# Two-layer hybrid encoder on one core: the transfers that sum the down weights, issued from GpSimd behind marks

## The chip, the cores and the metric

The kernel runs on one core of a Trainium2 chip. The core has five engines that run side by side, each with its own in-order queue: TensorE (PE, with its weight loads shown apart as PEld), VectorE (DVE), ScalarE (ACT), GpSimd (POOL) and SyncE (SP), which only issues transfers. Transfers run on 16 DMA engines, whoever issues them. The metric is the time of one execution on the device in microseconds (us).

## The reference

Two layers of a bidirectional encoder over 512 tokens of width 1024, all in float32. Each layer is a half-step feed-forward block (SwiGLU, inner width 2816), a mixer with three kinds of attention, and a second half-step feed-forward block, each between two RMS norms:

```python
for l in range(DEPTH):                       # 2
    y = swiglu(rmsnorm(h, ffn1_pre_g[l]), ffn1_w_gu[l], ffn1_w_down[l])
    h = h + 0.5 * rmsnorm(y, ffn1_post_g[l])
    u = rmsnorm(h, mix_pre_g[l])
    proj = u @ w_in[l]                       # q, k, v of A, B, C and the gates
    ...                                      # oa, ob, oc: three attentions
    yb = jnp.einsum('bsnc,ncd->bsnd', branches, w_branch[l])
    merged = jnp.sum(gates * yb, axis=2)
    h = h + rmsnorm(merged @ w_out[l], mix_post_g[l])
    y = swiglu(rmsnorm(h, ffn2_pre_g[l]), ffn2_w_gu[l], ffn2_w_down[l])
    h = h + 0.5 * rmsnorm(y, ffn2_post_g[l])

def swiglu(x, w_gu, w_down):
    gate, up = jnp.split(x @ w_gu, 2, axis=-1)
    return (jax.nn.silu(gate) * up) @ w_down
```

## The kernel before, in words

A product in float32 is made as three matmuls of a high and a low part (`mm3`, lines 291 to 293, and `unit`, line 1002): every weight tile is fetched (`wr`, three buffers, 512 KB each), copied to a high part by ACT (line 199) and to a low part by DVE (line 200), both in one buffer of tag `wp`, of which there are four.

The kernel is four feed-forward blocks and two mixers, in the order ffn(0,1), mixer 0, ffn(0,2), ffn(1,1), mixer 1, ffn(1,2). A feed-forward block computes its first `plain` of 22 rows of the inner layer straight (6 in the first block, 4 in the others), and the rest in `count` groups. Each group makes a gate and an up row by seven products of half size, a Strassen-like scheme (`product`, line 783, 84 matmuls of 256 columns in a group). Its weights are two `wr` tiles fetched by SP (`fetches`, line 186), summed and split on DVE and ACT (`sum13` line 637, `low1` line 645, `low24` line 674 and their like). `gated` (line 851) writes a row of activations at the end of a group. In the first block alone `keep` (lines 720 to 723) also turns the input by 32 transposes and stores it to memory (`kept<-h`, SP).

The down projection uses the same scheme, and there sums of weight quarters are wanted: `s3`, `s2`, `s1` and `s4`. They are not made on an engine but in memory. `sum_up(l, which)` returns 32 steps for a block: four sums, each of four copies (`begin_sum`, line 252, from the weights or from an earlier sum into a tile `sum`) and then four additions (`add_to`, line 256, a transfer from GpSimd's queue that adds into that tile), 512 KB each. All tiles `sum` have memory of their own. Later the sums are read like other weights (line 869).

Who calls the steps: `begin` of the first block fills `stream["beside"]` with the 32 steps of ffn(0,1), and the group loop takes three of them at a time (line 981). The mixer of layer l makes a list `todo` of the steps for ffn(l,2) and, in layer 0, for ffn(1,1) too, 64 and 32 steps, and spreads them over its own 77 steps (`ORDER`, line 1460). The place in the program is only where a step is traced: a scheduler writes each engine's order, outside of the regions under `ordered()`, by when it expects an instruction to be ready, and a copy of weights from memory is ready at once.

In a mixer GpSimd also multiplies for the rotary embedding: `rope` (lines 1247 to 1256) copies a projection on ACT, shifts it through four small SP transfers (`sh<-raw`), multiplies by a table on GpSimd (line 1255) and adds on DVE (line 1256). `combine` adds branches on GpSimd (line 1408).

Of the kernel before, what the change touches and what calls it, by code (L numbers as in the profile page):

```python
# [34 lines left out]
KP = KF - 2 * KS  # L35
# [74 lines left out]
def encoder_kernel(ctx: ExitStack, tc: tile.TileContext, order, xT, wts, cols, rows, rpb, consts, tables, out):  # L110
    nc = tc.nc
# [19 lines left out]
    def nm(s):  # L131
        serial[0] += 1
        return f"{s}{serial[0]}"

    def big(tag, dt=F32, shape=(P, T), name="v"):
        if tag in BUFS:
            return sb.tile(list(shape), dt, tag=tag, name=nm(name), bufs=BUFS[tag])
        kind, pool = phase[0]
        return pool.tile(list(shape), dt, tag=tag, name=nm(name), bufs=ABUFS[kind][tag])

    def small(tag, w=4, bufs=4):
        return sb.tile([P, w], F32, tag=tag, name=nm(tag), bufs=bufs)
# [4 lines left out]
    V, A, G, PE = nc.vector, nc.scalar, nc.gpsimd, nc.tensor  # L147

    def f(t):
        return t.bitcast(F32)  # L150
# [21 lines left out]
    stream = {"raw": [], "ready": [], "made": 0, "held": {}, "limit": 0, "stop": NTILES * 2, "later": [], "pace": 1, "eng": nc.scalar, "beside": []}  # L172
# [57 lines left out]
    extra, down, sums = [], {}, {}  # L230
# [5 lines left out]
    for l in range(L):  # L236
        for which in (1, 2):
# [3 lines left out]
            for key, (r, c) in places.items():  # L241
                src = wts[(NSTREAM + len(extra)) // WB].rearrange("p (a b) -> p a b", a=2)
# [3 lines left out]
    def sum_up(l, which):  # L246

        steps = []

        def begin_sum(key, old, u):  # L250
            t = dr.tile([P, 2, T], F32, tag="sum", name=nm("sum"), bufs=L * 2 * 4 * (KS // 2))
            nc.sync.dma_start(t, down[l, which, (old, u)] if old in ("21",) else sums[l, which, (old, u)])
            sums[l, which, (key, u)] = t

        def add_to(key, more, u):
            G.dma_start(sums[l, which, (key, u)], down[l, which, (more, u)], accum_op=ALU.add, max_dma_last_dim=4096)

        for key, old, more in (("s3", "21", "11"), ("s2", "s3", "22"), ("s1", "21", "22"), ("s4", "s2", "12")):
            steps.extend((lambda key=key, old=old, u=u: begin_sum(key, old, u)) for u in range(KS // 2))
            steps.extend((lambda key=key, more=more, u=u: add_to(key, more, u)) for u in range(KS // 2))  # L260
        return steps

    G.memset(ones, 1.0)
    G.memset(epst, EPS)
# [30 lines left out]
    def dense(blocks, X, tags=("mm",), i=None, accs=None, ws=None, midway=None, hooks={}):  # L295
        accs = accs or [bank(tags[n % len(tags)]) for n in range(len(blocks))]
        kept = []
        for k in range(len(X)):
            if midway and k == len(X) // 2:
                midway()  # L300
            x = X[k] if i is None else (X[k][0][:, i, :], X[k][1][:, i, :])
            for n, (acc, (name, l, r0, c)) in enumerate(zip(accs, blocks)):
                w = ws[k * len(blocks) + n] if ws else wblk(name, l, r0 + k, c)
                kept.append(w)
                mm3(acc if i is None else acc[:, HALVES[i]], w, x, k == 0, k == len(X) - 1)
            if k in hooks:
                hooks[k]()
        return (accs, kept) if i == 0 else accs

    def dense1(name, l, c, X, r0=0, tag="mm", midway=None):  # L310
        return dense([(name, l, r0, c)], X, (tag,), midway=midway)[0]
# [196 lines left out]
    def ffn(l, which, X, accs):  # L508
# [4 lines left out]
        plain = 6 if first else 4  # L513
# [39 lines left out]
        acts, low2, few = {}, [None, None], []  # L553
        PH, PL = [], []

        def place(m):
# [13 lines left out]
                acts[m] = low2[1][k // HK][:, :, k % HK, :]  # L570
            return acts[m]

        def settle(u):

            for parts in (PH, PL):
                if u < 2:
                    t = sb.tile([P, 2, T], F32R, tag="wp", name=nm("part"), bufs=BUFS["wp"])
                    parts.append([t[:, 0, :], t[:, 1, :]])
                else:
                    parts.append([big("t", F32R, name="part") for _ in range(2)])  # L580
            for k in range(2):
                p, q, a = PH[u][k], PL[u][k], few[0][:, 2 * u + k, :]
                A.activation(p, a, AF.Copy)
                V.tensor_tensor(out=q, in0=a, in1=f(p), op=ALU.subtract)
# [3 lines left out]
        def finish(m, pg, pu):  # L588
            t = big("t", name="t")
            if first:  # L590
                v = big("t", name="v")
                V.tensor_tensor(out=t, in0=pg, in1=rB, op=ALU.mult)
                A.activation(t, t, AF.Silu)
                V.scalar_tensor_tensor(out=v, in0=pu, scalar=-1.0, in1=rB, op0=ALU.mult, op1=ALU.mult)
                V.tensor_tensor(out=place(m), in0=t, in1=v, op=ALU.mult)
            else:
                A.activation(t, pg, AF.Silu)
                V.scalar_tensor_tensor(out=place(m), in0=pu, scalar=-1.0, in1=t, op0=ALU.mult, op1=ALU.mult)
# [154 lines left out]
        finish(1, g1, u1)  # L753
        for m in range(2, plain):
            finish(m, dense1(gu, l, m, X.blocks), dense1(gu, l, KF + m, X.blocks, tag="at"))
        while later:
            later.pop(0)()
        if first:
# [169 lines left out]
        for g in range(count):  # L928
            more, last = g + 1 < count, g + 1 == count
            p1(g)  # L930
            if g:
                add22(g - 1)
            low24(g)
            if more:
                high1(g + 1)
            seed(g)
            if more:
                sum13(g + 1)
            p7(g)
            if more:  # L940
                high13(g + 1)
                low1(g + 1)
            copy7(g)
            if g:
                p3(g - 1)
            if more:
                sum2(g + 1)
            else:
                preps(1)
            if g:  # L950
                silu1(g - 1)
            if more:
                high12(g + 1)
            if g:
                gated(g - 1)
            p6(g)
            if more:
                low13(g + 1)
            else:
                preps(2)  # L960
            copy2(g)
            p4(g)
            add21(g)
            if last:
                p5(g)
                add22(g)
                t3(0)
            p2(g)
            silu0(g)
            if more:  # L970
                low12(g + 1)
                sum4(g + 1)
                fetches(g + 2)
                p5(g)
                high24(g + 1)
            if g == count - 3:
                cut("1", "11", 0)
            if g == count - 2:
                cut("1", "11", 1)
                loads(3)  # L980
            for _ in range(3):
                if stream["beside"]:
                    stream["beside"].pop(0)()
        assert not stream["beside"]
        region = ordered()
        region.__enter__()
# [114 lines left out]
        for s, (kind, u) in enumerate(seq):  # L1101
# [28 lines left out]
            elif kind == "3" and u == 0:  # L1130
# [7 lines left out]
                for tb in range(2):  # L1138
# [4 lines left out]
                    t = kept_v["v12"][:, tb, :]  # L1143
# [115 lines left out]
    def mixer(l, op, first):  # L1259
        w, X = "w_in", op.blocks  # L1260
        todo = sum_up(l, 2) + (sum_up(l + 1, 1) if l + 1 < L else [])
# [7 lines left out]
        for c0, n in ((0, 512), (512, 384)):  # L1269
            m = big("g", name="mask")  # L1270
# [158 lines left out]
        def do(u):  # L1429
            kind, i = u[:2], int(u[2:] or 0)  # L1430
            if kind == "qa":
                if i == 0:
                    held[u] = qkv_a(*first)
                else:
                    early = second if i == 1 else []
                    late = [dense1(w, l, c + i, X) for c in (QA, KA, VA)[len(early) :]]
                    held[u] = qkv_a(*early, *late)
            elif kind == "kb":
                held["kb"] = qkv_b(KB), turn(plain(dense1(w, l, VB, X), False), 2)
            elif kind == "qb":  # L1440
                held[u] = qkv_b(QB + i)
            elif kind == "qc":
                held[u] = qkv_c(i)
            elif kind == "aa":
                attn_a(i, *held.pop(f"qa{i}"))
            elif kind == "ab":
                attn_b(i, held.pop(f"qb{i}"), *held["kb"])
            elif kind == "ac":
                attn_c(*held.pop(f"qc{i}"))
            elif kind == "fc":  # L1450
                finish_c(i)
            elif kind[0] == "g":
                gates("abc".index(kind[1]), i)
            elif kind[0] == "y":
                combine("abc".index(kind[1]), kind[1], i)

        steps = ORDER.split()
        for n, u in enumerate(steps):
            do(u)
            while todo and len(todo) * (len(steps) - 10) > (len(steps) - 10 - n) * todo_n:  # L1460
                todo.pop(0)()
        assert not todo
        M = [split(merged[m], "st", 0.5) for m in range(KD)]

# [113 lines left out]
```

## Time and profile before

| What | Value |
|---|---|
| median of 3 runs | 2659.02 us (2656.55 to 2659.67) |
| the profiled execution | 2658.71 us, span 2656.9 us |
| PE, PEld busy | 2466.7 us (93%), 2165.6 us (82%) |
| DVE, ACT, POOL busy | 1766.8 us (66%), 1349.2 us (51%), 139.6 us (5%) |
| mean granted PE clock | 0.965 |
| moved by transfers | 390.93 MB, mean 147 GB/s |

The profile is of one execution. The page gives, for each of 40 equal slices of the span (66.4 us), one digit, the busy share in tenths. Other views group the instructions by line or by the tile that they write, list who waited for whom, follow the chain of work that ended last back from the end, and give the queues of the DMA engines, where q0 holds GpSimd's transfers, q1 SP's and q10 ACT's. A busy PE is not PE at its peak, since matmuls overlap: how long a run of them takes is read from the chain.

### The profile page before, as it was taken

To read this page: it belongs to the slowest core of one execution; us is meant where nothing else is said; L and a number is where in the kernel's file an instruction comes from. 1 tells how busy PE (TensorE), PEld (TensorE's weight loads), DVE (VectorE), ACT (ScalarE), POOL (GpSimd) and SP (SyncE) were. 2 spreads that over 40 slices of the span, in tenths; PEclk is the share of its full clock that TensorE was granted. 3 is DMA by queue.
4 is the path that set the end of the run, shared out by engine and by line. 5 is a ranking of instruction groups with operands and counts; after the bars stand their busy time and mean duration, and the time that the engine had idled before them with its cause. 6 is when DMAs were issued, how large, how long until landed. Compare 5 with 4: busy or idle time off the path is not lost.

```text
span 2656.9 us, 37791 instructions
## 1 busy us (share of the span) xinstructions
PE 2466.7 (93%) x14298; PEld 2165.6 (82%) x14298; DVE 1766.8 (66%) x2903; ACT 1349.2 (51%) x2471; POOL 139.6 (5%) x128
## 2 busy tenths in 40 slices
PE   7367799899999999999999999989999999999997
PEld 6257798788887787999878999877888778799986
DVE  6144577667676655788766787657577574678784
ACT  4122355455555545555555556446555454555553
POOL 1111100000001110000000000000001111000000
PEclk9678899999999999999999999999999999999999
DMA  9999946364453333333542335636344433333452
GB/s 283 270 292 287 245 130 228 110 179 108 118 154 106 110 102 113 98 103 110 198 159 96 104 104 170 202 121 168 108 120 130 120 111 102 98 111 104 135 185 93
DMA packets 129430, 390.93 MB, mean 147 GB/s; under 512 B 17504, under 2 KB 24288, under 8 KB 128224
## 3 DMA queue, kind: packets, MB, share of 16 engines
q1 hardware_dynamic: 98000, 275.18, 32.3%
q10 hardware_dynamic: 22032, 79.78, 9.9%
q0 software_dynamic: 9216, 33.56, 6.6%
q8 instruction: 112, 1.84, 0.3%
q14 instruction: 70, 0.57, 0.1%
HBM read 335.50 MB, written 81.79 MB: 157 GB/s over the span
## 4 chain that ended last, share of the span: by engine, by line
PE 69%; DMA 13%; DVE 9%; ACT 4%; issue 2%; SPq 1%; POOL 1%; DVEq 0%; ACTq 0%; POOLq 0%
PE mm L783 20%; PE mm L1002 7%; PE mm L293 7%; PE mm L292 7%; PE mm L291 7%; DMA sum<-in_wts_dram 6%; PE at L1002 4%; PE at L783 3%; DMA wr<-in_wts_dram 3%; PE at L293 2%; PE at L292 2%; PE at L291 2%; PE o L1002 2%; DMA sh<-raw 1%; DMA braw<-in_rpb_dram 1%
## 5 line engine op out<-in xcount | busy, mean ns | idle before, releaser
L291 PE MATMUL mm<-X,w 128*128 128x512 f32 (+1 forms) x998 | 386.1, 387 | 2.4 <-ACT w L199 1.2
L292 PE MATMUL mm<-X,w 128*128 128x512 f32 (+1 forms) x998 | 386.0, 387 | 0.0
L293 PE MATMUL mm<-X,w 128*128 128x512 f32 (+1 forms) x998 | 384.6, 386 | 0.0
L200 DVE TENSOR_TENSOR w<-wr,w 128x512 fp32r<-128x512 f32 x366 | 258.9, 714 | 186.5 <-ACT w L199 183.1
L199 ACT ACTIVATE w<-wr 128x512 fp32r<-128x512 f32 x366 | 226.5, 627 | 239.9 <-PE mm L293 176.7
L783 PE MATMUL mm<-ht,h 128*128 128x256 f32 x1120 | 323.4, 289 | 16.1 <-ACT at L822 13.5
L783 PE MATMUL mm<-lt,h 128*128 128x256 f32 x1120 | 322.2, 288 | 0.0
L783 PE MATMUL mm<-ht,l 128*128 128x256 f32 x1120 | 322.1, 288 | 0.0
L783 PE MATMUL mm<-X,h 128*128 128x256 f32 x1120 | 213.3, 288 | 44.5 <-DVE v L837 44.5
L783 PEld LDWEIGHTS mm<-ht,h 128*128 128x128 f32 x1120 | 220.9, 197 | 17.1 <-ACT at L822 14.1
L783 PEld LDWEIGHTS mm<-lt,h 128*128 128x128 f32 x1120 | 221.0, 197 | 0.0
L783 PEld LDWEIGHTS mm<-ht,l 128*128 128x128 f32 x1120 | 220.5, 197 | 0.0
L291 PEld LDWEIGHTS mm<-X,w 128*128 128x128 f32 x998 | 190.9, 191 | 33.9 <-ACT w L199 1.4
L783 PEld LDWEIGHTS mm<-X,h 128*128 128x128 f32 x1120 | 179.0, 196 | 46.0 <-DVE v L837 45.7
L293 PEld LDWEIGHTS mm<-X,w 128*128 128x128 f32 x998 | 190.6, 191 | 31.6
L292 PEld LDWEIGHTS mm<-X,w 128*128 128x128 f32 x998 | 191.0, 191 | 31.0
L1002 PE MATMUL mm<-wh,f 128*128 128x512 f32 x640 | 199.7, 390 | 0.0
L783 PE MATMUL mm<-X,l 128*128 128x256 f32 x560 | 161.0, 287 | 0.0
L637 DVE TENSOR_TENSOR r<-wr,wr 128x1024 f32<-128x1024 f32 x70 | 85.5, 1221 | 87.5 <-DMA wr<-in_wts_dram 83.6
L1002 PEld LDWEIGHTS mm<-wh,f 128*128 128x128 f32 x640 | 120.2, 188 | 25.0
L645 DVE TENSOR_TENSOR l<-wr,h 128x1024 fp32r<-128x1024 f32 x70 | 85.7, 1225 | 80.9 <-PE mm L783 80.9
L1002 PE MATMUL mm<-wl,f 128*128 128x512 f32 x320 | 125.0, 391 | 3.6 <-DVE wl L880 3.6
(348 smaller groups left out, 5463.4 us busy)
## 6 DMA issues: line engine op xcount, KB each, us to landing
wr<-in_wts_dram SPq DMA_DIRECT2D x187, 512.0 KB, 3.6
wr<-in_wts_dram ACTq DMA_DIRECT2D x152, 512.0 KB, 3.7
sum<-in_wts_dram POOLq DMA_DIRECT2D x64, 512.0 KB, 18.2
sum<-in_wts_dram SPq DMA_DIRECT2D x32, 512.0 KB, 10.4
sum<-sum SPq DMA_DIRECT2D x32, 512.0 KB, 7.6
ht<-sum SPq DMA_DIRECT2D x32, 512.0 KB, 4.3
lt<-sum SPq DMA_DIRECT2D x32, 512.0 KB, 4.4
ht<-in_wts_dram SPq DMA_DIRECT2D x28, 512.0 KB, 4.5
```

The source lines that it names most:

```text
L199: A.activation(hi, raw, AF.Copy)
L200: V.tensor_tensor(out=lo, in0=raw, in1=f(hi), op=ALU.subtract)
L291: PE.matmul(acc, w[0], x[0], start=start, stop=False)
L292: PE.matmul(acc, w[0], x[1], start=False, stop=False)
L293: PE.matmul(acc, w[1], x[0], start=False, stop=stop)
L637: V.tensor_tensor(out=W[g]["r13"], in0=base, in1=raws[g][0], op=ALU.add)
L645: V.tensor_tensor(out=W[g]["l1"], in0=raws[g][0], in1=f(W[g]["h1"]), op=ALU.subtract)
L783: PE.matmul(acc, ws[i], xs[j], start=start and k == n == 0, stop=stop and k == HK - 1 and n == 2, skip_group_check=True,)
L1002: PE.matmul(acc, x[i], w[j], start=start and n == 0, stop=stop and n == 2, skip_group_check=True)
```

## The change

The copies that begin a sum are issued by GpSimd, on the queue of the additions, in place of SP. A new function `paced` makes a mark on GpSimd, a copy of one column (128 x 1) of data that the running step has just made, and puts the transfers that it is given behind that mark in GpSimd's order (`issue_after` orders the issue on that engine and adds no other wait). In the first block two steps go behind a row of activations after each of the four plain rows from m = 2, and two after each group from g = 1, so that the 32 steps end with the 16th pair. In the mixers the steps that fall due after a step of `ORDER`, mostly one in mixer 0 and one in every second step in mixer 1, go behind a mark read from the low part of the weight tile that was used last.

```diff
         def begin_sum(key, old, u):
             t = dr.tile([P, 2, T], F32, tag="sum", name=nm("sum"), bufs=L * 2 * 4 * (KS // 2))
-            nc.sync.dma_start(t, down[l, which, (old, u)] if old in ("21",) else sums[l, which, (old, u)])
+            G.dma_start(t, down[l, which, (old, u)] if old == "21" else sums[l, which, (old, u)])
             sums[l, which, (key, u)] = t
...
+    def paced(calls, src):
+
+        mark = G.tensor_copy(small("mark", 1, 2), src)
+        with tc.issue_after(mark.ins):
+            for call in calls:
+                call()
...
+        def beside(src):
+            if stream["beside"]:
+                paced(stream["beside"][:2], src)
+                del stream["beside"][:2]
...
         for m in range(2, plain):
             finish(m, dense1(gu, l, m, X.blocks), dense1(gu, l, KF + m, X.blocks, tag="at"))
+            beside(acts[m][:, 0:1])
...
-            for _ in range(3):
-                if stream["beside"]:
-                    stream["beside"].pop(0)()
+            if g:
+                beside(acts[plain + g - 1][:, 0, 0:1] if plain + g > KP else acts[plain + g - 1][:, 0:1])
...
         for n, u in enumerate(steps):
             do(u)
+            ready = []
             while todo and len(todo) * (len(steps) - 10) > (len(steps) - 10 - n) * todo_n:
-                todo.pop(0)()
+                ready.append(todo.pop(0))
+            if ready:
+                paced(ready, f(stream["tile"][1])[:, 0, 0:1])
```

## The prediction

> **What bounds the kernel now.** I read the page first: busy shares by slice, and the transfers' share under them.
>
> ```profile
> span 2656.9 us, 37791 instructions
> ...
> PE   7367799899999999999999999989999999999997
> ...
> DMA  9999946364453333333542335636344433333452
> ```
>
> TensorE's digit is 8 or 9 everywhere but in the first five slices of 66 us and at the very end, and in those five the 16 DMA engines are full. So I asked for busy time in stretches: the first feed-forward block up to its last product (15 to 390), then the two mixers, with a later feed-forward block between them.
>
> ```profile
> 15.00:390.00 375.00, 258.13 (x1703) 242.50 (x1702) 184.86 (x259) 125.71 (x212) 52.28 (x64) 0.82 0.92 256
> ...
> 530.00:1045.00 515.00, 505.88 (x2464) 414.65 (x2462) 335.83 (x753) 278.08 (x604) 43.44 (x29) 1.00 0.44 125
> 1045.00:1260.00 215.00, 212.32 (x1627) 206.42 (x1628) 167.29 (x214) 119.27 (x194) 0.00 (x0) 0.98 0.34 102
> ...
> 1760.00:2255.00 495.00, 484.63 (x2379) 397.68 (x2380) 322.56 (x724) 264.59 (x570) 43.49 (x29) 0.99 0.44 125
> ```
>
> The columns are length, busy time of PE, PEld, DVE, ACT and POOL, granted clock, DMA share, GB/s. In the first block PE is idle for 117 us of 375 and its clock is 0.82. In the other three stretches PE is busy 98% of the time with DMA at 0.34 to 0.44. What fills the DMA engines is told by the tile `sum`:
>
> ```profile
> L256 POOL DMA_DIRECT2D sum<-in_wts_dram x64: 805/814/976, 24.2 to 302.1; - x64
> L252 SPq DMA_DIRECT2D sum<-in_wts_dram x32: 488/581/1156, 15.3 to 268.9; - x32
> L252 SPq DMA_DIRECT2D sum<-sum x32: 467/474/607, 31.9 to 290.3; - x32
> ```
>
> All 128 transfers of all four feed-forward blocks, 64 additions and 64 copies, start between 15 and 302 us, though three of the blocks need theirs only much later. The waits of that stretch say whom this hurts:
>
> ```profile
> DVE r L637 <- DMA wr<-in_wts_dram: 78.0, 11, 18.4
> ...
> PE o L720 <- ACT h L722: 50.9, 3, 30.5
> DVE t L592 <- DMA kept<-h: 45.3, 2, 38.3
> PE mm L783 <- DVE v L837: 44.5, 6, 15.0
> ...
> SPq L252 <- DMA sum<-in_wts_dram: 146.8, 23, 30.9
> ```
>
> The last row is SP's queue: for 146.8 us it stood at a copy that waited for an addition to land, and the stores `kept<-h` and the loads `wr` stood behind it. PE's two waits, 50.9 and 44.5 us, are the ends of those two chains.
>
> **What stage one would take without it.** PE's work that is left at 60 us comes from a row of busy time for line 293 alone, the transposes' row, and three links of the chain that ended last:
>
> ```profile
> 60.00:150.00 90.00, 16.58 (x38) 8.13 (x38) 0.70 1.02 274
> ```
>
> ```profile
> L720 PE MATMUL o<-cons,a x32: 270/296/475, 55.5 to 126.4; 128*128 128x128 f32 x32
> ```
>
> ```profile
> 377.16 10.08 PE mm L783 x84
> 387.24 1.45 PE at L783 x12
> ...
> 428.03 23.12 PE mm L1002 x102
> ```
>
> Of line 293's matmuls 38 come after 60 us, and as many of 291 and 292: 114 of 512 columns. In an unbroken run 102 of that width take 23.12 us, 0.227 each: 25.8 us. A product matmul takes 10.08/84 = 0.12 us; the 32 transposes at the same price make 3.8. A group is 84 products, 10.08 us, and there are 16 groups (22 rows less 6 plain ones): 161.3. So 60 + 25.8 + 3.8 + 161.3 = 251 us, against 388.7 (387.24 + 1.45) now. At most **137.7 us** can be had.
>
> **What the DMA engines would have to carry.** Two answers on the queues and issues, the first of a quiet stretch (1100 to 1250), the rest of a full one (160 to 300):
>
> ```profile
> q1 hardware_dynamic: 4359, 15.89, 34.6%
> ...
> wr<-in_wts_dram SPq DMA_DIRECT2D x30, 512.0 KB, 3.6
> ```
>
> ```profile
> q0 software_dynamic: 4332, 15.77, 59.0%
> q1 hardware_dynamic: 3144, 24.50, 45.1%
> ...
> sum<-in_wts_dram POOLq DMA_DIRECT2D x32, 512.0 KB, 18.2
> wr<-in_wts_dram SPq DMA_DIRECT2D x16, 512.0 KB, 11.8
> sum<-sum SPq DMA_DIRECT2D x16, 512.0 KB, 9.7
> sum<-in_wts_dram SPq DMA_DIRECT2D x14, 512.0 KB, 13.2
> ```
>
> A weight load costs all 16 engines 0.346 x 150/30 = 1.73 us. An addition: 0.59 x 140 us over 15.77/0.524 = 30 of them, 2.74 us. The copies share q1 with 16 loads: 0.451 x 140 - 16 x 1.73 = 35.4 us over 30, 1.2 us each. Three blocks' 48 additions and 48 copies leave stage one: 131.5 + 57.6 = 189 us of engine time, of 0.92 x 375 = 345. What stays, 156 us, fits into 251 at a share of 0.62, so PE becomes the bound. The stores and loads lose the queue in front of them; next late is a load that meets a pair of sums.
>
> **The pairs that stay (16 of them).** Four run beside the plain products, twelve beside groups. The groups have little room, as the chain and VectorE's order show:
>
> ```profile
> 277.46 12.13 DMA wr<-in_wts_dram
> ...
> 294.05 11.37 DMA wr<-in_wts_dram
> ...
> 311.12 7.91 DMA wr<-in_wts_dram
> ```
>
> ```profile
> 1152.05 1.23 DVE L645 TENSOR_TENSOR l<-wr,h 128x1024 fp32r<-128x1024 f32 x1 [1.56 <-PE mm L783]
> 1153.19 0.69 DVE L851 TENSOR_TENSOR a<-t,v 128x512 f32<-128x512 f32 x1
> ```
>
> From load to load it is 16.59 and 17.06 us, of which the load 12.13 and 11.37; the rest (sum, splits, release of the buffer) is 4.5 to 5.7, say 5.1. A group of 10.08 us is kept if a load lands within 5.0 us; quietly it takes 3.6. The release is L645's end, and L851, whose output the mark reads, comes right behind it: the pair of sums and the load always meet. If they don't slow each other: 0. If the load waits for the whole pair: 3.6 + 2 x 2.74 + 5.1 = 14.2 for an addition pair (+4.1), 3.6 + 2.4 + 5.1 = 11.1 for a copy pair (+1.0), six of each: 31 us. The load starts ahead and both interleave, so I take half: **15 us**. The four plain pairs stand beside loads issued two tiles ahead: 3 us, ends 0 and 10. Stage one ends at 251 + 18 = 269: **-119.7 us**.
>
> **The parts with one answer.** SP loses 64 issues of some 0.5 us; POOL gains them at an addition's 0.81, 64 x 0.81 = 52 us over stretches where it is busy 43 of 515 or, with the additions gone elsewhere, not at all: nothing on PE's path. The 112 marks (16 + 64 + 32) read one column each; the nearest POOL rows are an issue, 0.81, and the 1.3 of a whole tile below, and I take 0.2; POOL's idle time hides them. In the first block only sums stand behind a mark. An addition waits for a copy issued two pairs (some 20 us) earlier in the groups, four steps in a mixer, and copies land in 9.7 even when all is full: no wait.
>
> **The mixers.** The first gets 64 transfers: 32 x 3.94 = 126 us of engine time, share 0.44 to 0.68; the second 32: 0.44 to 0.57. PE has 2% to spare. Behind POOL's new work stands the rotary step. First who waits for it (line 1256 on VectorE: us, times), then one such link of the chain, then two of POOL's multiplies in order of time:
>
> ```profile
>   POOL sh L1255: 24.2, 14
> ```
>
> ```profile
> 833.83 3.57 DMA sh<-raw
> 837.55 1.30 POOL sh L1255
> ```
>
> ```profile
> 697.67 1.29 POOL L1255 TENSOR_TENSOR sh<-sh,sinR 128x512 f32<-128x512 f32 x1 [36.01 <-DMA sh<-raw]
> ...
> 762.15 1.28 POOL L1255 TENSOR_TENSOR sh<-sh,sinR 128x512 f32<-128x512 f32 x1 [13.62 <-DMA sh<-raw]
> ```
>
> 14 of the 26 rotary steps are waited for. At worst each meets an issue in front of it (0.81) and an addition beside its `sh` transfer (2.74): 14 x 3.55 = 50 us. At best none does: 0. A transfer is in flight a quarter of the time in the first mixer (126/515) and POOL is issuing a tenth: 14 x (0.25 x 2.74 + 0.1 x 0.81) = **11 us**. Each mark also holds a weight buffer (`wp`, four of them) until POOL has read it; a buffer lasts PE 12 matmuls, 2.7 us, so four hold 10.9, and the low part that the mark reads is written before PE uses it. I take nothing; if that cover goes, see the last rival.
>
> **Sum.** The profiled execution took 2658.7 us (span 2656.9), 0.3 under the median of 2659.0. 2658.7 - 119.7 + 11 = **2550 us**.
>
> The Trainium skill's page "DMA: Bandwidth & Descriptors", section "Issuing engines are not separate DMA queues", says that issuing from several engines "will only save the time on the sequencer it takes to initiate the DMA". By it the move to POOL alone is worth SP's 64 issues, about 32 us off the path, and all gain has to come from the delay; SP's 146.8 us row speaks for more, since a wait on the queue moves along with the issue. The same page ("SWDGE vs HWDGE vs iDMA") calls SP's path the faster to set up, and says that GpSimd writes its descriptors where VectorE can lock it out. That speaks against the change; the issues' 805 to 976 ns beside a VectorE busy half the time show little of it, and by its figures to the first byte, about 1 us against 0.6, 64 copies would be 26 us later in all, beside other work.
>
> **Rivals.** (a) The stage stays bound by transfers: its own sums cost the full 31 + 10 us, and some stores stay late; PE's wait goes to `wr` again. The overlap of L645 and L851 speaks for it, a share of 0.62 against. 2658.7 - 137.7 + 41 + 11 = 2573, to 2590 if a third of the 50.9 us wait stays. (b) The mixers pay in full: 50 us instead of 11, 2589. For it speaks their 2% of slack, against it that transfers are in flight only a quarter of the time. (c) Slower: marks keep weight buffers. POOL works in order; a mark queued behind a rotary multiply that waits for its transfer (36.0 and 13.6 us above) is read late, the split of a later tile can't start, PE stops. With 13.6 us of wait and 8 of cover (three buffers), each of 26 steps costs 5.6: 146 us, more than the 119.7 won, 2685. It decides from 4.6 us a step. Against it: those waits are mostly idle time, in which a mark may go first. (d) The marks don't hold the transfers back, as their data come early: 2658. Against it: in the mixers the data are that step's weights, which can't be there in stage one.
>
> **How the numbers follow.** Main case 0.63 (2521, the full 137.7 with free mixers, to 2572), (a) 0.17, (b) 0.12, (c) 0.06, (d) 0.02. Range: 2520 to 2605, which takes in (a), (b) and a mix of their bounds; main case's own 2521 to 2572. Faster by over 0.2% 0.92, within 0.2% (about what a measurement of this kernel can tell from no change) 0.02, slower 0.06.
>
> **What would show it.** Right: about 30 `sum` issues before 280 us, the rest inside the mixers; the DMA digit falls to 6 or 7 in the first four slices and rises in the first mixer; last L783 at 260 to 285; `DVE t <- kept` gone; `wr` landing in 4 to 7 us beside pairs. The forecast is wrong if `wr` waits stay above 40 us in stage one, if PE's idle time in the mixers grows past 60 us, or if ACT's split (L199) waits for POOL.

## The result and the profile after

The changed kernel takes 2569.86 us (median of four runs, 2564.52 to 2575.61), the kernel before 2657.8 in the same sitting (2656.55 to 2659.67): a ratio of 0.967, interval 0.9647 to 0.9691. The forecast was 2550, within 2520 to 2605. The profiled run is the highest of the four, 2575.61 us with a span of 2573.8.

From the page, the rows that answer to those of before:

```profile
span 2573.8 us, 37991 instructions
...
PE   8999989999899999999989999899999999999997
...
DMA  5686636677558533335523346365565553233452
```

The full DMA digits of the first five slices (now 64 us each) are 5 to 8, PE's first digits are 8 and 9, and the transfers are back in the slices of the two mixers. Busy time up to the last product of the first block (columns as before: length, PE, PEld, DVE, ACT, POOL, clock, DMA share, GB/s):

```profile
15.00:254.50 239.50, 229.59 (x1703) 218.57 (x1702) 183.53 (x258) 125.86 (x211) 40.90 (x48) 0.98 0.67 190
```

The same 1703 matmuls that took 375 us with PE idle for 117 now take 239.5, with PE idle for 10 and the clock at 0.98. The tile `sum` (issue times in ns, first and last start) shows the transfers spread, and all of them on GpSimd:

```profile
L256 POOL DMA_DIRECT2D sum<-in_wts_dram x64: 801/839/1544, 79.3 to 2103.5; - x64
L252 POOL DMA_DIRECT2D sum<-in_wts_dram x32: 488/514/1062, 53.3 to 1949.3; - x32
L252 POOL DMA_DIRECT2D sum<-sum x32: 488/512/633, 110.7 to 2069.6; - x32
```

The waits between 15 and 300 us (engine, line, what it waited for: us in total, times, longest):

```profile
POOL mark L265 <- DVE a L864: 97.8, 12, 13.4
POOL mark L265 <- DVE ap L607: 82.0, 4, 46.0
...
DVE r L649 <- DMA wr<-in_wts_dram: 14.9, 7, 4.8
...
PE o L732 <- ACT h L734: 4.0, 1, 4.0
PE mm L796 <- DVE v L850: 3.5, 3, 2.9
```

The waiting has moved from SP's queue, which other work needs, to GpSimd's marks, behind which only sums stand. The load wait of 78.0 us is 14.9, PE's two waits of 50.9 and 44.5 us are 4.0 and 3.5, and `DVE t<-kept` is gone.

The time is then best told in stretches: stage one up to the first block's last product, and each mixer from the last matmul of the down projection before it to the first product behind it. In us:

| | before | after | difference |
|---|---|---|---|
| stage one | 389.8 | 254.5 | -135.3 |
| first mixer | 590.9 | 631.8 | +40.9 |
| second mixer | 590.2 | 609.0 | +18.8 |
| the groups of the three later blocks | 3 x 181.3 | 3 x 178.0 | -9.9 |
| four down projections | 472.5 | 477.3 | +4.8 |
| the rest, by difference | | | -2.4 |
| span | 2656.9 | 2573.8 | -83.1 |

Stage one gave more than forecast, and the mixers took back 59.7 us where 11 were forecast. Their rows of busy time, first of the kernel after, then of before:

```profile
373.20:1005.00 631.80, 591.13 (x2857) 487.77 (x2856) 384.40 (x824) 316.00 (x672) 99.97 (x157) 0.96 0.59 167
...
1652.80:2261.90 609.10, 578.86 (x2857) 477.91 (x2857) 384.58 (x824) 315.57 (x671) 71.31 (x93) 0.98 0.52 146
```

```profile
507.70:1098.60 590.90, 573.69 (x2856) 475.45 (x2855) 383.68 (x824) 315.81 (x672) 43.44 (x29) 0.99 0.42 122
...
1752.30:2342.50 590.20, 572.21 (x2856) 473.30 (x2855) 384.49 (x824) 315.69 (x672) 43.49 (x29) 0.99 0.42 122
```

In the first mixer PE's idle time went from 17.2 to 40.7 us (+23.5), and its busy time for the same matmuls from 573.7 to 591.1 (+17.4) at a clock of 0.96 instead of 0.99. In the second it is +12.2 and +6.7. So a loss has two parts, a stall and what follows it. One stall, by four stretches around it and then by the chain that ended last (start, length, what):

```profile
460.00:469.30 9.30, 9.30 (x52) 7.78 (x50) 4.60 (x12) 4.20 (x10) 0.00 (x0) 1.00 1.02 258
469.30:474.10 4.80, 0.03 (x1) 0.00 (x0) 3.59 (x13) 2.32 (x7) 0.00 (x0) 0.73 0.16 46
474.10:478.50 4.40, 4.37 (x18) 3.81 (x18) 2.93 (x8) 1.69 (x4) 0.00 (x0) 0.52 0.83 193
478.50:484.00 5.50, 5.50 (x34) 4.66 (x32) 5.10 (x12) 3.67 (x9) 0.00 (x0) 1.00 0.40 92
```

```profile
457.67 12.78 DMA braw<-in_rpb_dram
...
474.82 0.43 PE mm L298
...
478.74 0.24 PE mm L299
...
685.11 10.19 DMA sw<-hi
...
773.69 9.23 DMA sh<-raw
```

The DMA engines are full up to 469.3; a 256 KB bias `braw` lands only after 12.78 us; PE does nothing for 4.8 us; then for 4.4 us its granted clock is 0.52 and a matmul of 512 columns takes 0.43 us instead of 0.24. The other two links are the same story with other small transfers. Eight idle gaps of 1.8 to 5.3 us inside the mixer make 28 us; the kernel before has none of 2 us or more there but the two at the mixer's ends, which both kernels have. The Trainium skill's page "TensorE: Matmul & The Clock Gate" (section "Part 1: The HAM clock gate") says that an idle window of about 3.4 us halves the clock until about as long a busy one has passed. A half clock behind the 4.8 us fits that, but this trace does not need so long a gap: at 0.73 on average over the gap, the halving began 2.2 us into it, and all eight gaps were followed by half clock, the two shortest, of 1.8 and 1.9 us, too. The row behind the one of 1.8 us, which ended at 648.5:

```profile
649.00:652.40 3.40, 3.40 (x12) 2.92 (x12) 3.28 (x11) 1.82 (x3) 0.00 (x0) 0.50 0.67 154
```

Nor is the length of a gap a sure sign: one of 2.3 us in the second mixer (at 1876) had a clock of 1.00 behind it.

### The profile page after: what moved, and what is told of

It reads as the page before. It is cut to its first block, busy times and chain, and to the rows that moved or that the text cites. A ratio compares the mean times of both kernels' runs of the same rounds, so it can differ in the third digit from the quotient of the medians.

```text
span 2573.8 us, 37991 instructions
## 1 busy us (share of the span) xinstructions
PE 2454.7 (95%) x14298; PEld 2147.6 (83%) x14298; DVE 1766.9 (69%) x2903; ACT 1350.9 (52%) x2471; POOL 212.6 (8%) x304
## 4 chain that ended last, share of the span: by engine, by line
PE 72%; DVE 10%; DMA 8%; ACT 5%; SPq 2%; issue 2%; POOL 1%; ACTq 0%; DVEq 0%; POOLq 0%
PE mm L796 22%; PE mm L1014 7%; PE mm L300 7%; PE mm L298 7%; PE mm L299 7%; PE at L1014 4%; PE at L796 4%; DMA sh<-raw 3%; PE at L300 2%; PE at L299 2%; PE at L298 2%; DMA wr<-in_wts_dram 2%; DMA braw<-in_rpb_dram 2%; PE o L1014 2%; DVE w L200 1%
## 5 line engine op out<-in xcount | busy, mean ns | idle before, releaser
L796 PE MATMUL mm<-ht,h 128*128 128x256 f32 x1120 | 316.6, 283 | 2.4 <-ACT at L835 2.4
L796 PE MATMUL mm<-lt,h 128*128 128x256 f32 x1120 | 315.7, 282 | 0.0
L796 PEld LDWEIGHTS mm<-ht,h 128*128 128x128 f32 x1120 | 213.5, 191 | 2.6 <-ACT at L835 2.6
L796 PEld LDWEIGHTS mm<-ht,l 128*128 128x128 f32 x1120 | 213.5, 191 | 0.0
L796 PEld LDWEIGHTS mm<-lt,h 128*128 128x128 f32 x1120 | 213.2, 190 | 0.0
L796 PE MATMUL mm<-X,h 128*128 128x256 f32 x1120 | 200.6, 279 | 3.5 <-DVE v L850 3.5
L796 PEld LDWEIGHTS mm<-X,h 128*128 128x128 f32 x1120 | 171.0, 189 | 4.4 <-DVE v L850 4.1
L796 PE MATMUL mm<-X,l 128*128 128x256 f32 x560 | 155.3, 277 | 0.0
L265 POOL COPY mark<-w 128x1 f32<-128x1 f32 x96 | 26.1, 272 | 1421.3 <-DVE w L200 1418.7
```

The costliest lines, as they stand in the source:

```text
L265: mark = G.tensor_copy(small("mark", 1, 2), src)
L796: PE.matmul(acc, ws[i], xs[j], start=start and k == n == 0, stop=stop and k == HK - 1 and n == 2, skip_group_check=True,)
```

## The experiments

The theory after the result: sums beside a mixer delay the small transfers on its chains, and beside feed-forward blocks they cost little. The rivals were the marks themselves (a weight buffer held, GpSimd's queue in front of the rotary multiply), the bursts in which sums are issued, and the shape of the transfers. Ratios are to the kernel before, run on the same chip in the same sitting.

**Sums beside their own blocks.** Every block takes its own 32 steps (the line moves out of the part that the first block alone runs); the mixers have none.

```diff
-            stream["beside"] = sum_up(l, which)
...
+        stream["beside"] = sum_up(l, which)
...
-        todo = sum_up(l, 2) + (sum_up(l + 1, 1) if l + 1 < L else [])
+        todo = []
```

> Every block makes its own 32 sum transfers beside its own plain rows and groups, in pairs behind marks as the first block does in the changed kernel; the mixers issue none. Transfer theory (the sums in flight make the mixers' small transfers land late, 41 + 19 us in the two mixers): the mixers go back to 591 and 590 us, and each of the three later blocks pays what the first one pays, 0 to 5 us: 2570 - 60 + 3 to 15 = 2513 to 2525 us. Rival, groups as tight as the prediction had them (1.3 us of room for a weight load): 15 us in each later block, 2555 us. Rival, the mixers' loss is no matter of the sums but of another order of work: mixers stay above 600 us, 2570 or more.

Measured: 2530.31 us, ratio 0.9536 (0.9519 to 0.9552), faster than the change itself and 5 us above the range of the transfer theory. Its first mixer, and its tile `sum`:

```profile
371.10:961.90 590.80, 574.64 (x2856) 475.07 (x2855) 383.75 (x823) 315.23 (x672) 44.77 (x32) 0.99 0.43 124
```

```profile
L256 POOL DMA_DIRECT2D sum<-in_wts_dram x64: 797/862/1166, 80.6 to 2355.9; - x64
```

The mixers are back at 590.9 and 589.1 us, PE idle 16 of the first; the groups of the later blocks are 181.4, 183.6 and 180.4, that is 3.4, 5.6 and 2.4 above the 178.0 of the changed kernel. So the 96 transfers of the later blocks cost 11 us beside the groups (15 in a second run below) and 60 beside the mixers. In the rotary chain's transfer (KB each, median us from issue to landing) one sees the difference, after, before and here:

```profile
sh<-raw SPq DMA_DIRECT2D x52, 64.0 KB, 4.4
```

```profile
sh<-raw SPq DMA_DIRECT2D x52, 64.0 KB, 2.2
```

```profile
sh<-raw SPq DMA_DIRECT2D x52, 64.0 KB, 2.0
```

**The same, with the mixers' marks kept but nothing behind them.**

```diff
-        todo = []
+        todo = [None] * (64 if l + 1 < L else 32)
...
-                paced(ready, f(stream["tile"][1])[:, 0, 0:1])
+                paced([], f(stream["tile"][1])[:, 0, 0:1])
```

> As the run before it, with the 64 and 32 marks of the mixers kept, and no transfer behind them. Transfer theory: a mark costs nothing without its transfer, the time is that of the run without marks within 4 us. Rival, queue theory (marks hold weight buffers, or stand in front of the rotary multiply): a good part of the 60 us comes back, 20 us or more over the run without marks.

Measured: 2530.46 us, 0.9541 (0.9527 to 0.9555). First its marks (ns minimum, median, maximum), then its first mixer:

```profile
L265 POOL COPY mark<-w x96: 179/183/704, 408.7 to 2053.2; 128x1 f32<-128x1 f32 x96
```

```profile
374.40:967.40 593.00, 575.91 (x2857) 475.83 (x2856) 385.78 (x824) 314.92 (x670) 58.04 (x96) 0.99 0.42 123
```

The mixers take 593.0 and 590.6 us with ninety-six marks on weight buffers. Without marks they took 590.9 and 589.1 above and 591.0 and 592.4 in a second run (below), so a cost of the marks is not shown. The marks are not what the mixers pay for; the transfers are. This run takes the transfers' issue on GpSimd away too. But in the changed kernel only four of the 26 rotary multiplies stood right behind other work on GpSimd: before 22 it had been idle, before 18 of them until `sh<-raw` landed (121.0 us in all). So the transfers in flight, and not their issue in front of the multiply, make most of the delay in the rotary chain; `braw` and `sw` don't pass GpSimd at all.

**Only the 96 others leave; the first block's own sums are as before.** `sum_up` takes the engine as an argument, and the loop of the first block is the old one.

```diff
-            stream["beside"] = sum_up(l, which)
+            stream["beside"] = sum_up(l, which, nc.sync)
...
-            beside(acts[m][:, 0:1])
...
-            if g:
-                beside(acts[plain + g - 1][:, 0, 0:1] if plain + g > KP else acts[plain + g - 1][:, 0:1])
+            for _ in range(3):
+                if stream["beside"]:
+                    stream["beside"].pop(0)()
```

> The first block's own 32 transfers as before the change (copies on SP, three steps a group, no marks), the mixers' 96 as after it. Tells leaving from pacing in stage one. If leaving of the 96 is what counts: 248 us of sums' engine time fall to 63, all of them in the first 100 us, where they still stand in front of the stores and loads on SP; stage one ends at 265 to 300 instead of 254, in all 2580 to 2615 us. If pacing and the other queue count as much: stage one ends above 320, 2635 or more.

Measured: 2591.6 us, 0.978 (0.976 to 0.9801). Stage one ends at 272.4 us: leaving of the 96 is worth 117.4 (2.7 of them a faster product, see the last run), the pacing of the own pairs, with their copies' move to GpSimd, another 17.9. The row of busy time up to that end, then the chain:

```profile
15.00:272.40 257.40, 232.31 (x1699) 219.47 (x1698) 183.63 (x258) 126.54 (x212) 13.13 (x16) 0.95 0.59 176
```

```profile
52.19 20.00 DMA sum<-in_wts_dram
...
73.87 14.43 DMA kept<-h
```

SP's queue still stood behind an addition for 20 us, and the store `kept<-h` behind it. Without pairs beside them the 16 groups of this block take 158.6 us from first to last product, against 166.7 with twelve pairs in the changed kernel: the pairs cost 8 us.

**Only the mixers' sums are early, on SP; the first block's are paced.**

```diff
-        todo = sum_up(l, 2) + (sum_up(l + 1, 1) if l + 1 < L else [])
+        todo = sum_up(l, 2, nc.sync) + (sum_up(l + 1, 1, nc.sync) if l + 1 < L else [])
...
-                paced(ready, f(stream["tile"][1])[:, 0, 0:1])
+                for call in ready:
+                    call()
```

> The first block's own 32 paced on GpSimd as after the change, the other 96 as before it (copies on SP, no marks, so they can all start early). Leaving theory: stage one stays bound by transfers, ends at 360 to 390, mixers at 591: 2630 to 2660 us. If pacing the first block's own pairs carries a good part of the gain: below 2610 us.

Measured: 2602.16 us, 0.9812 (0.9794 to 0.983). The time lies below 2610, but not as the pacing theory had it, and it separates less than it was meant to. Its copies from weights on SP, and a wait between 15 and 470 us:

```profile
L252 SPq DMA_DIRECT2D sum<-in_wts_dram x24: 488/578/1111, 198.6 to 431.6; - x24
```

```profile
PE at L1014 <- ACT wh L889: 20.3, 1, 20.3
```

The early sums start only at 199 us. Their additions stand on GpSimd behind the first block's marks, and SP's order has their first copies behind the loads up to then, though no wait holds them there; why the scheduler put them so late the trace does not tell. They hit the last groups (stage one 285.7, +31 on the changed kernel) and the first down projection (174.1 us against 118.6, +56) instead; the mixers are clean (589.1 and 590.1).

**The queue alone: all on GpSimd, no marks.**

```diff
     def paced(calls, src):
-        mark = G.tensor_copy(small("mark", 1, 2), src)
-        with tc.issue_after(mark.ins):
-            for call in calls:
-                call()
+        for call in calls:
+            call()
```

> The copies moved to GpSimd's queue, no marks, all transfers free to start early. Delay theory: all 128 still crowd stage one, PE is bound by transfers until 330 to 390 us: 2600 to 2665 us. The skill's rule, that the issuing engine saves issue time alone: no change from before within 0.5%, 2640 to 2665. Queue theory (SP's 147 us of standing behind copies are the loss): stores and loads are free, stage one ends near 300, 2570 to 2600 us.

Measured: 2634.65 us, 0.9922 (0.9903 to 0.9942). Stage one is 367.6 us, 22 shorter than before, and the mixers are untouched (590.4 and 591.0). Its row of busy time, its additions, and what is waited for between 15 and 400 us:

```profile
15.00:367.60 352.60, 269.49 (x1742) 252.32 (x1742) 190.46 (x269) 130.65 (x222) 79.17 (x120) 0.85 0.96 271
```

```profile
L256 POOL DMA_DIRECT2D sum<-in_wts_dram x64: 805/827/1118, 8.8 to 312.7; - x64
```

```profile
ACT w L670 <- DMA wr<-in_wts_dram: 66.7, 13, 8.2
...
PE mm L794 <- DVE v L848: 36.2, 12, 5.9
```

All 128 transfers still start ahead of 313 us and keep the DMA engines at a share of 0.96; the loads now wait for those engines, and SP no longer stands at a copy. That is the delay theory's forecast. The rule that only issue time is saved said less than 0.5%, and 0.8% came; the queue theory's 2570 to 2600 is out. So, taken in this order, the move to GpSimd's queue is 22 of the 135.3 us in stage one and the delay behind marks the rest; whether the 22 are issue time or SP's waits is not told apart.

**Smaller pieces of the copies** (4 KB rows; the additions had them already).

```diff
-            G.dma_start(t, down[l, which, (old, u)] if old == "21" else sums[l, which, (old, u)])
+            G.dma_start(t, down[l, which, (old, u)] if old == "21" else sums[l, which, (old, u)], max_dma_last_dim=4096)
```

> The changed kernel with the copies cut into 4 KB pieces, as the additions are, instead of 32 KB pieces. Rival in the transfer theory: a small transfer of a mixer waits behind whole 32 KB pieces of a copy. Then the two mixers fall from 632 and 609 us by 15 to 30 together. If it is the engine time of the sums, the additions' above all, that makes them wait, the mixers stay within 8 us of that, or lose a little as copies take longer.

Measured: 2561.72 us, 0.9649 (0.9632 to 0.9667), mixers 621.5 and 606.5. That is 10.3 and 2.5 us less than in the changed kernel's first profile, but 2.5 and 1.2 less than in its second (below). An effect of a few us is possible and not shown.

**Sums only beside the dense steps of a mixer**, at most two at a time, never beside attention heads, where one weight tile stays the newest for several steps. GpSimd's order in the changed kernel shows what that removes (start, length, instruction, idle before it):

```profile
455.64 0.19 POOL L265 COPY mark<-w 128x1 f32<-128x1 f32 x1 [27.88 <-DVE w L200]
...
456.14 0.85 POOL L256 DMA_DIRECT2D sum<-in_wts_dram  x1 [0.31 <-issue]
456.82 1.15 POOL L256 DMA_DIRECT2D sum<-in_wts_dram  x1
457.49 1.54 POOL L256 DMA_DIRECT2D sum<-in_wts_dram  x1
```

Three additions go within 2 us, ahead of the `braw` load at 457.67 above.

```diff
-            if ready:
+            if u[0] not in "gy":
+                todo[:0] = ready
+            elif ready:
+                todo[:0] = ready[2:]
+                ready = ready[:2]
                 paced(ready, f(stream["tile"][1])[:, 0, 0:1])
```

> The changed kernel, but in the mixers the sums that fall due wait for the next gate or branch projection step, at most two behind one mark; none is issued behind a step of attention, whose marks are all ready at once. Burst theory (three or four sums together behind marks that read the same weight tile make the long waits of 9 to 13 us): the first mixer falls from 632 to 600 to 615 us, the second from 609 to 592 to 600. If any sum beside an attention head costs the same, whether alone or in a burst: above 620 and above 603.

Measured: 2570.99 us, 0.9687 (0.9672 to 0.9703), mixers 626.8 and 609.6. Its chain, then GpSimd's order:

```profile
563.21 8.68 DMA sh<-raw
...
683.57 10.67 DMA sw<-hi
```

```profile
535.00 1.04 POOL L252 DMA_DIRECT2D sum<-sum  x2
...
536.63 1.72 POOL L256 DMA_DIRECT2D sum<-in_wts_dram  x2 [0.26 <-issue]
...
542.81 1.02 POOL L252 DMA_DIRECT2D sum<-in_wts_dram  x2
```

Leaving out the marks behind attention steps gains nothing: the same small transfers are late and the loss is the same. But the edit did not thin the sums out. With two single additions between these rows, eight transfers went within 9 us, since the marks of several dense steps come ready close together. So the run does not decide whether bursts are what makes a sum costly.

**The changed kernel and the first variant again, and two finer variants.**

> The changed kernel once more, on the chip of the three beside it: 2562 to 2578 us.

Measured: 2565.96 us, 0.9675 (0.9662 to 0.9688), mixers 624.0 and 607.7, stage one 254.9. The mixers' loss is 33 and 18 us here, 41 and 19 in the first profile. In the first mixer PE is idle as long as before (40.8 us against 40.7): six of the eight gaps come again, for 22.2 us instead of 23.2, and two are shorter. What differs is the clock behind the gaps, 0.98 instead of 0.96 over the mixer, and so PE's busy time, 583.2 us instead of 591.1.

> Each block's sums beside its own groups, once more, as the base of the next two: 2520 to 2535 us.

Measured: 2530.38 us, 0.9541 (0.9526 to 0.9556). The groups are 182.7, 182.9 and 183.0 us. From its chain, at the first group of the second feed-forward block:

```profile
968.99 6.98 DMA wr<-in_wts_dram
```

One load of 6.98 us there leaves PE idle for 3.0 us, and the next 10 us run at a mean clock of 0.85. Each of the other two blocks has one such gap, of 3.08 and 3.26 us, likewise at an early group, and no other above 1 us. So a block's 4.7 to 5.0 us over 178.0 are one stall at its first pairs and the slower clock behind it, and the other pairs hide. To begin the pairs a group later was not tried.

Then each pair in the blocks is one addition and one copy, in place of two of a kind:

```diff
-        for key, old, more in (("s3", "21", "11"), ("s2", "s3", "22"), ("s1", "21", "22"), ("s4", "s2", "12")):
+        for key, old, more in (("s3", "21", "11"), ("s1", "21", "22"), ("s2", "s3", "22"), ("s4", "s2", "12")):
...
+        steps = copies[:2]
+        for c, a in zip(copies[2:], adds):
+            steps.extend((a, c))
+        return steps + adds[-2:]
```

> As the run before it, with the order of the sums changed to s3, s1, s2, s4 and the pairs made of one addition and one copy each (3.9 us of engine time in place of 5.5 and 2.4). If two additions beside a weight load are what stretches a group, most of the 11 us that the three later blocks pay (181.4, 183.6 and 180.4 against 178.0) goes: 8 us less than that run. If any pair costs the same: within 3 us of it.

Measured: 2531.79 us, 0.9535 (0.9519 to 0.9551): no gain over two of a kind, groups 182.9, 182.8 and 182.5.

> As the run before it, with the copies cut into 4 KB pieces. In the mixers that was worth some 13 us of 60. If a weight load, too, waits behind 32 KB pieces, the groups gain another 2 to 5 us; if not, no difference beyond 3 us.

This is the last one with the copies in 4 KB rows. Measured: 2524.91 us, 0.9523 (0.9509 to 0.9536), the fastest kernel of all; its interval overlaps those of the others with sums beside their own blocks, so the finer edits are not shown to matter. The kernels of this kind beat the one before by 4.6 to 4.8%; three of them ran beside the change's second run and are 1.3 to 1.6% under its 2565.96.

**Why do product groups take less?** In every kernel with marks a group takes 9.89 us and in those without 10.08, in blocks where nothing was changed. The kernel before, with the marks' two buffers allocated and cleared once, nothing more:

```diff
+    for _ in range(2):
+        G.memset(small("mark", 1, 2), 0.0)
```

> The kernel before the change with one thing added: two buffers of the mark's 4 bytes a partition, each cleared once at the start; no mark, no transfer moved. In every run with marks a group of products took 9.89 us (178.0 us for 18) and a 512-column matmul 0.229 us, in both runs without marks 10.08 us (181.3) and 0.227. If where the tiles lie in memory, shifted by the mark's buffers, sets this: 178.0 and 0.229 here, and a total within 5 us of the kernel before. If it takes the marks' running or less crowded transfers: 181.3 and 0.227.

Measured: 2657.37 us, 1.0013 (1.0003 to 1.0024). Chain rows of product matmuls, first of the changed kernel, then of this one:

```profile
1101.26 8.47 PE mm L796 x72
```

```profile
1156.94 8.64 PE mm L785 x72
```

That is 117.6 and 120.0 ns a matmul. The presence of the buffers alone is not the cause, and the cause stays open. The changed kernel's down projections go the other way, 102 matmuls of 512 columns in 23.33 us instead of 23.12:

```profile
292.99 23.33 PE mm L1014 x102
```

## Why the prediction held, and which of its steps did not

- **What bound stage one.** Right. The 96 sums of other blocks filled the DMA engines and held SP's queue; without them PE is the bound (idle 10 us of 239.5). The transfers that stay were put at 156 us of the DMA engines' time, and 0.67 of 239.5, 160 us, were measured. The wait of SP's queue, though, 146.8 us in its row, was read as speaking for a gain of its own; the run on the queue alone shows that the move, wait and issue together, was worth only 22 us. That is within the 32 us that the prediction worked out for the issues alone by the Trainium skill's page "DMA: Bandwidth & Descriptors" (section "Issuing engines are not separate DMA queues"), though the run does not show that issue time is what was saved.
- **The most that could be had.** 251 forecast as the end of stage one without any pairs. The first block's groups began at 87.8 us (254.5 less 166.7) where the sum has 92.6 (60 + 25.8 + 3.8 + 3 for the plain pairs), and without pairs they take 158.6 where it has 161.3.
- **The own pairs.** Forecast 18 us, of which 15 in the groups; 8 were measured there, at a faster product. "A load must land within 5.0 us" was too strict. Loads beside pairs landed in 5.6 us (median, 120 to 250 us) and most groups kept their pace, as this chain row, a group of 84 in 9.91 us beside its pair, shows:

```profile
242.00 9.91 PE mm L796 x84
```

  The 5.1 us taken for the rest of a load's loop came from links in a stretch that was itself held up by transfers, which is likely why it was too long. Stage one ended at 254.5 instead of 269.
- **The marks.** Put at nothing: 0.18 us each on weights, and nobody waits for one; the two mixers with marks alone take 1183.6 us, two runs without them 1180.0 and 1183.4. Right, and rival (c), slower through held weight buffers, is out, as is (d).
- **The mixers.** This term was mis-sized: 11 us forecast, with ends 0 and 50, and 59.7 measured (50.6 in the second profile). The sums' load was right: 126 us of engine time forecast for the first mixer, and 125 measured (0.59 of 631.8 us less 0.42 of 590.9). What a meeting costs was not. Three things were left out. It counted one kind of chain, the rotary `sh`, and there are also the bias `braw` and the stores and loads `st` and `sw`. It took a meeting as an addition of 2.74 us in a quarter of the cases, but sums come several at once (what the bunching alone costs is not shown) and a transfer of 64 KB can take 9.23 us. And it priced a stall at its own length, while here each is followed by some us at half the clock: PE's busy time grew by 17.4 of the first mixer's 40.9 us, and by 1.0 in the run without sums there (574.64 against 573.69). The prediction's own sign, PE idle in the mixers for over 60 us, did appear: 70.9 us in both, from 35.2. Rival (b), the mixers paying in full, is what came true, and was hidden in the total by the 15 us more of stage one and the 10 us of the groups. That the total came so near is in part luck: the faster groups were in no term of the prediction, and their cause is open.
- **The sum.** 2550 to the profiled 2575.6: -14.5 in stage one (254.5 for 269), +48.7 in the mixers, -9.9 in later groups, and 1.3 for what is left.

## What to carry to other kernels

A transfer that nobody needs yet is issued at once by a scheduler that sees it ready; to hold it back, tie its issue to data of the step beside which it should run, from an engine whose queue holds little else. Put it beside a stage whose own transfers are large and prefetched (96 transfers cost 11 and 15 us there in two runs), not beside one whose chain of dependent work runs through small transfers (60 and 51 us), and count all the small transfers on that chain, not one kind. Price a stall of TensorE with the half clock that may follow it: here all eight stalls of 1.8 to 5.3 us had one, and two profiles of one kernel differed by 8 us in a mixer through it, at the same idle time.

## What the hardware showed

- After an idle gap of 4.8 us the granted clock was 0.52 for 4.4 us, and after one of 1.8 us 0.50 for 3.4 us; the clock row of a whole mixer (0.96 for 0.99) tells how much time goes that way.
- A plain copy is issued by GpSimd in 0.51 us (median), where SP took 0.58 and 0.47; an addition takes 0.84. GpSimd was no slower at this.
- A mark of one column took 0.18 us on a weight tile and 1.05 us on an activation tile (the same form, 128x1 f32). What differs is VectorE beside it: all twelve marks of 1.05 us started 0.2 us after an instruction of VectorE that reads two inputs (L665) and ended within 0.05 us of its end, and most of the slower marks on weights ended with a VectorE instruction in the same way. That VectorE holds GpSimd up was not tested. The two groups, then one such pair:

```profile
L265 POOL COPY mark<-w x96: 175/186/902, 408.5 to 2103.0; 128x1 f32<-128x1 f32 x96
L265 POOL COPY mark<-a x12: 1046/1047/1048, 109.8 to 219.3; 128x1 f32<-128x1 f32 x12
```

```profile
109.55 1.22 DVE L665 TENSOR_TENSOR l<-r,h 128x1024 fp32r<-128x1024 f32 x1
...
109.76 1.05 POOL L265 COPY mark<-a 128x1 f32<-128x1 f32 x1 [13.44 <-DVE a L864]
```

- The pace of matmuls differed between programs by 2% (117.6 and 120.0 ns a matmul), in blocks whose code was not changed.
